# One level of Strassen's seven products for w_down, in three phases among the gate/up tiles of a decoder block

## The chip, the core and the metric

The kernel runs on one core of a Trainium2 chip. The metric is the device time of one execution in microseconds (us), as the median of several runs. The engines named below are TensorE (PE), which multiplies matrices and has a separate row for loading the stationary operand (PEld), VectorE (DVE), ScalarE (ACT), GpSimd (POOL) and SyncE (SP). SP's queue issues the transfers between the chip's memory (HBM) and the on-chip memory (SBUF); matmuls write to PSUM, of eight banks of 512 fp32 columns.

## The reference

One decoder layer on 512 tokens of width 1024, in float32: a mixer of state-space heads and pooling groups, a cross-attention into 256 memory tokens, a gated feed-forward, each behind an RMS norm and with a residual sum, and a final norm. What the change touches is the last part:

```python
D_MODEL, SEQ, D_FF = 1024, 512, 2816

def rmsnorm(x, g):
    y = x * lax.rsqrt(jnp.mean(x * x, axis=-1, keepdims=True) + EPS)
    return y * g

def swiglu(u, w_gate_up, w_down):
    gate, up = jnp.split(u @ w_gate_up, 2, axis=-1)
    return (jax.nn.silu(gate) * up) @ w_down

h = h + hybrid_mixer(rmsnorm(h, mix_norm), ...)
h = h + memory_cross_attention(rmsnorm(h, xattn_norm), rmsnorm(mem, mem_norm), ...)
h = h + swiglu(rmsnorm(h, ffn_norm), w_gate_up, w_down)
return rmsnorm(h, final_norm)
```

## The kernel before

**Layout.** Features lie on partitions, in tiles of 128; the 512 tokens are the free dimension. The residual stream is eight tiles h1 of 128 x 512. Every product is done in a reduced float32 format (fp32r) to nearly full precision: each operand is split in a high part (a cast) and a low part (the rest), and each product of 128 x 128 by 128 x 512 is three matmuls, high x high, high x low and low x high (`mm3`, L105).

**Weights.** They come in units of 128 x 1024 fp32. `load_unit` (L137) starts a transfer from SP into a raw buffer (three of them, `wb[0]`), and `split_unit` (L143) makes the high part `whi` by a cast on ACT (four buffers) and the low part `wlo` by a subtraction on DVE (five buffers). `advance` (L1091) runs one slot ahead of the matmuls.

**The order.** `SPEC` is a list of slots; each slot names items such as `f:3` (gate/up tile 3) or `d:2` (output tile 2 of the down projection). An item has matmuls (`mm`) and work behind them (`post`). The recording order of slot t is: the posts of slot t - 1, the weights of slot t + 1, then the matmuls of slot t. A scheduler then sets the order on each engine. Every engine, and SP's queue, works its own list in order.

**Feed-forward.** `i_ff` (L975) makes a tile of 128 features of the gate and of the up projection (48 matmuls), multiplies both by the norm's factor, applies SiLU and multiplies (DVE), and splits the result into `ffh` and `ffl`. There are 22 such tiles. Then `i_down` (L998) makes eight output tiles of 128 x 512 over all 22 reduction tiles, 66 matmuls each, with the weights stationary. Its post adds the tile to h1, squares it on ACT and adds the squares up on DVE. The eighth tile is cut in two halves of 256 tokens (`dA`, `dB`), and `i_final` (L1033) makes the final norm for each half: a matmul with ones sums the squares over features (`Rms`, L213), and ACT and DVE make the factor. The first half's norm and output run beside the second half's matmuls.

**What the loads before the feed-forward need.** The pairs of state-space heads, `P:0` to `P:7`, hold their decay matrices in buffers tagged m and m2, two of each. `i_op` (L740) loads the residual's x tiles again from SP, one per output tile.

Of the kernel before, what the change touches and what calls it, by code (L numbers as in the profile page):

```python
# [7 lines left out]
F32 = mybir.dt.float32  # L8
# [38 lines left out]
]  # L47
# [3 lines left out]
def hybrid_block(ctx: ExitStack, tc: tile.TileContext, a: dict, out: bass.AP,  # L51
                 act_bufs=69, la=1, wb=(3, 4, 5), eng="", dact=(0, 1), raw_n=6, warm=12, spec=None, start=START, smm=START_MM, hu=1, dbg=None):
    nc = tc.nc
# [80 lines left out]
    def add_unit(key, ap, n):  # L134
        units[key] = (ap, n)

    def load_unit(key):  # L137
        ap, n = units[key]
        raw = wraw.tile([P, 1024], F32, tag="raw", name=nm("raw"))
        nc.sync.dma_start(raw[:, :n], ap)  # L140
        ready[key] = raw

    def split_unit(key):  # L143
        n = units[key][1]
        raw = ready[key]
        hi = whi_p.tile([P, 1024], F32R, tag="hi", name=nm("whi"))
        lo = wlo_p.tile([P, 1024], F32R, tag="lo", name=nm("wlo"))
        nc.scalar.copy(hi[:, :n], raw[:, :n])  # L148
        yield
        nc.vector.tensor_tensor(out=lo[:, :n], in0=raw[:, :n], in1=hi.bitcast(F32)[:, :n], op=ALU.subtract)  # L150
        ready[key] = (hi, lo)
        yield
# [42 lines left out]
    DS = ((0, 8), (8, 16), (16, 22))  # L195
    for m in range(8):
        for i, (k0, k1) in enumerate(DS):
            add_unit(("d", m, i), a["w_d"][m, :, k0 * P:k1 * P], (k1 - k0) * P)

# [13 lines left out]
    class Rms:  # L213
# [27 lines left out]

        def first(self):
            self.ps = PS(self.base)
            self.pre = rms4[0].pre
            nc.tensor.matmul(self.ps[:, :self.n], ones, st[self.acc][:, self.o:self.o + self.n],
                             start=True, stop=False)

        def second(self, sq):
            nc.tensor.matmul(self.ps[:, :self.n], ones, sq, start=False, stop=True)

        def post(self):
# [31 lines left out]

# [1 line left out]
    rms1 = Rms("r1", "xacc", parts=False)  # L285

    def i_start(its):
# [58 lines left out]
        return it  # L346

    def i_out():
        def post():
            for m in range(8):  # L350
                nc.sync.dma_start(out[m * P:(m + 1) * P, :], st["hg", m][0].bitcast(F32))

        return Item(post=post)

# [122 lines left out]

# [1 line left out]
    def i_btm(g):  # L479
# [203 lines left out]

# [1 line left out]
    def i_v(m):  # L685
# [73 lines left out]
    rms3 = Rms("r3", "h2acc")  # L759
    rms4 = [Rms("r4a", "h3acc", 256, 0, False), Rms("r4b", "h3acc", 256, 256, False)]  # L760
    rmsm = Rms("rm", "macc", MEM)
# [19 lines left out]

# [1 line left out]
    def i_memld():  # L783
# [189 lines left out]

# [1 line left out]
    def i_ff(j):  # L975
        it = Item(keys=[("g", j), ("u", j)])

        def mm():
            xs = [st["fg", k] for k in range(8)]
            it.pg = PS("g")  # L980
            proj(it.pg, ready[("g", j)], xs)
            it.pu = PS("u")
            proj(it.pu, ready[("u", j)], xs)

        def post():
            yield from need("r3")
            g = mul("g", it.pg, st["r3",])
            nc.scalar.activation(g, g, AF.Silu)
            u = mul("u", it.pu, st["r3",])
            yield  # L990
            nc.vector.tensor_tensor(out=u, in0=u, in1=g, op=ALU.mult)
            yield
            yield from splits([("ff", j)], [("ff", 512)], [u])

        it.mm, it.post = mm, post
        return it

    def i_down(m, half=None, ks=(0, JF)):  # L998
        it = Item(keys=[("d", m, i) for i in range(3)] if not half and ks[0] == 0 else [])
        cs = slice(0, S) if half is None else slice(256 * half, 256 * half + 256)  # L1000
        last = ks[1] == JF

        def mm():
            if ks[0] == 0:
                st["dps", half] = PS("d")
            ps = st["dps", half][:, cs]
            for i, (k0, k1) in enumerate(DS):
                wh, wl = ready[("d", m, i)]
                for k in range(max(k0, ks[0]), min(k1, ks[1])):
                    o = slice((k - k0) * P, (k - k0 + 1) * P)  # L1010
                    xh, xl = st["ff", k]
                    mm3(ps, wh[:, o], wl[:, o], xh[:, cs], xl[:, cs], k == 0, k == JF - 1)
            if last and half is not None:
                rms4[half].first()

        def post():
            h = st["h1", m][:, cs]
            nc.vector.tensor_tensor(out=h, in0=h, in1=st["dps", half][:, cs], op=ALU.add)
            if half is not None:
                sq = T("sq", n=256)  # L1020
                st["sq7", half] = sq
                st["h3acc", "sq"] = nc.scalar.activation(sq, h, AF.Square)
            else:
                sq_acc("h3acc", h)
                nc.scalar.activation(h, h, AF.Identity, scale=col(V_FIN + m))
                if m == 6:
                    drain(rms4[0].split(KT - 1))

        it.mm = mm
        it.post = post if last else None  # L1030
        return it

    def i_final(half):  # L1033
        cs = slice(256 * half, 256 * half + 256)

        def post():
            yield from rms4[half].post()
            r = st["r4" + "ab"[half],]
            for m0, n in ((0, 1), (1, 1), (2, 2), (4, 2), (6, 2)):
                o = T("out").rearrange("p (m t) -> p m t", m=2)  # L1040
                for i in range(n):
                    m = m0 + i
                    h = st["h1", m][:, cs]
                    if m < 7:
                        nc.vector.tensor_tensor(out=o[:, i, :], in0=h, in1=r, op=ALU.mult)
                    else:
                        nc.vector.scalar_tensor_tensor(out=o[:, i, :], in0=h, scalar=col(V_FIN + 7), in1=r,
                                                       op0=ALU.mult, op1=ALU.mult)
                nc.sync.dma_start(out[m0 * P:(m0 + n) * P, cs].rearrange("(m p) t -> p m t", p=P), o[:, 0:n, :])
                yield  # L1050

        return Item(mm=lambda: rms4[half].second(st["sq7", half]), post=post)

    def rm(r):
        return Item(mm=r.mm, post=r.post)

# [1 line left out]
    x0, x1 = i_xbc(0), i_xbc(1)  # L1058
# [3 lines left out]
    def num(t):  # L1062
# [7 lines left out]
        "r2": lambda: rm(rms2), "rt": i_r2t, "q": i_q, "S": i_score, "T": i_ptr, "V": i_v2, "O": i_pv,  # L1070
        "o": i_o, "r3": lambda: rm(rms3), "f": i_ff, "d": i_down, "dA": lambda: i_down(7, 0),
        "dB": lambda k0, k1: i_down(7, 1, (k0, k1)), "F": i_final, "out": i_out,
    }
# [89 lines left out]
def _pack(inp):  # L1163
# [31 lines left out]
    w_u = np.stack([f(t) for t in u])  # L1195
    w_d = np.stack([f(mtile(g["w_down"], m)) for m in range(8)])
    dtp = np.zeros((KT, P, 96), z32)
# [24 lines left out]
    vecs[:, V_RC:V_RC + 16] = (1.0 / np.arange(1, 17)).astype(z32)  # L1222
    return {"xT": f(x.T), "memT": f(mem.T), "vecs": vecs, "w_dt": w_dt, "w_u": w_u, "w_d": w_d}

# [15 lines left out]
```

## Time and profile before

| what | us |
| --- | --- |
| runs of the kernel (3) | 832.57, 830.25, 832.3 |
| median | 832.3 |
| span of the profiled execution, first to last instruction | 828.6 |
| granted TensorE clock over the span | 0.996 of full |

The profile is of one execution. Of this execution the span is recorded; the time of a run lies a few us above it, 3.7 us at the median. The lines that matter are shown in the prediction. To read them: L106 is line 106 of the kernel; `d<-t_ffh,whi` is a matmul into PSUM tile d from the moving tile t_ffh and the stationary tile whi; x198 is a count; in rows of groups the busy time is followed by the mean duration of one in ns, then the idle time before the group and what ended it. Matmul records overlap, so their spacing has to be read from their starts.

### The profile page before, as it was taken

What the parts mean: (1) busy time and instruction counts of PE and PEld (TensorE: products, weight loads), DVE (VectorE), ACT (ScalarE), POOL (GpSimd) and SP (SyncE); (2) the same over time, 40 slices, a digit from 0 to 9 for tenths busy, and PEclk for the clock granted to TensorE, in tenths of its full rate; (3) what the DMA queues carried; (4) which work ended last, traced back from release to release, by engine and by line L of the source; (5) the groups of instructions that cost most, each with busy time, mean ns of one, the idle gap of its engine ahead of it and who ended that gap; (6) DMA issues with size and microseconds to landing.
All of it is one profiled execution on the core that took longest, in us unless ns stands there. A gap on an engine that the chain in (4) does not pass through costs nothing.

```text
span 828.6 us, 10051 instructions
## 1 busy us (share of the span) xinstructions
PE 816.6 (99%) x3926; PEld 686.8 (83%) x3926; DVE 505.5 (61%) x727; ACT 388.3 (47%) x600; POOL 1.7 (0%) x10
## 2 busy tenths in 40 slices
PE   9999999999999999999999999999999999999995
PEld 7878888888888899888888888888888888888885
DVE  7989978999866885447646544444444444232324
ACT  8668699477844563345534532233222332232221
POOL 0000000000000000000000000000000000000000
PEclk9999999999999999999999999999999999999998
DMA  7243514243262244223322233222323223333302
GB/s 264 78 152 102 171 62 144 70 163 120 103 221 86 76 155 160 92 77 127 102 77 91 87 102 102 94 88 98 102 101 102 88 85 96 96 96 102 100 1 101
DMA packets 31246, 89.77 MB, mean 108 GB/s; under 512 B 3664, under 2 KB 8144, under 8 KB 31200
## 3 DMA queue, kind: packets, MB, share of 16 engines
q1 hardware_dynamic: 31200, 89.15, 33.0%
q8 instruction: 30, 0.49, 0.3%
q14 instruction: 16, 0.13, 0.1%
HBM read 87.01 MB, written 2.13 MB: 108 GB/s over the span
## 4 chain that ended last, share of the span: by engine, by line
PE 91%; DVE 4%; ACT 2%; DMA 1%; issue 1%; SPq 0%; DVEq 0%
PE d L106 5%; PE d L108 5%; PE d L107 5%; PE u L107 5%; PE g L107 5%; PE u L106 5%; PE g L106 5%; PE u L108 5%; PE g L108 5%; PE v L107 2%; PE v L108 2%; PE v L106 2%; PE op L106 2%; PE op L108 2%; PE q L106 2%; PE q L107 2%
## 5 line engine op out<-in xcount | busy, mean ns | idle before, releaser
L148 ACT CAST whi<-raw 128x1024 fp32r<-128x1024 f32 x144 | 149.4, 1040 | 332.4 <-issue 108.0
L150 DVE TENSOR_TENSOR wlo<-raw,whi 128x1024 fp32r<-128x1024 f32 x144 | 173.5, 1207 | 109.6 <-ACT whi L148 109.5
L106 PE MATMUL d<-t_ffh,whi 128*128 128x512 f32 (+1 forms) x198 | 72.7, 367 | 0.0
L108 PE MATMUL d<-t_ffh,wlo 128*128 128x512 f32 (+1 forms) x198 | 72.3, 365 | 0.0
L107 PE MATMUL d<-t_ffl,whi 128*128 128x512 f32 (+1 forms) x198 | 72.3, 365 | 0.0
L106 PE MATMUL g<-t_fgh,whi 128*128 128x512 f32 x176 | 68.5, 389 | 0.0
L107 PE MATMUL g<-t_fgl,whi 128*128 128x512 f32 x176 | 68.5, 389 | 0.0
L108 PE MATMUL g<-t_fgh,wlo 128*128 128x512 f32 x176 | 68.5, 389 | 0.0
L106 PE MATMUL u<-t_fgh,whi 128*128 128x512 f32 x176 | 68.5, 389 | 0.0
L107 PE MATMUL u<-t_fgl,whi 128*128 128x512 f32 x176 | 68.5, 389 | 0.0
L108 PE MATMUL u<-t_fgh,wlo 128*128 128x512 f32 x176 | 68.5, 389 | 0.0
L277 DVE TENSOR_TENSOR t_u<-u,t_r3t 128x512 f32<-128x512 f32 x22 | 15.2, 691 | 69.0 <-PE u L108 69.0
L107 PEld LDWEIGHTS d<-t_ffl,whi 128*128 128x128 f32 x198 | 37.3, 189 | 6.1
L106 PEld LDWEIGHTS d<-t_ffh,whi 128*128 128x128 f32 x198 | 37.3, 189 | 6.0
L108 PEld LDWEIGHTS d<-t_ffh,wlo 128*128 128x128 f32 x198 | 37.3, 189 | 6.0
L277 DVE TENSOR_TENSOR t_g<-g,t_r3t 128x512 f32<-128x512 f32 x22 | 15.2, 691 | 44.3 <-PE g L108 44.3
L106 PEld LDWEIGHTS g<-t_fgh,whi 128*128 128x128 f32 x176 | 33.1, 188 | 6.9
L108 PEld LDWEIGHTS u<-t_fgh,wlo 128*128 128x128 f32 x176 | 33.1, 188 | 6.9
L106 PEld LDWEIGHTS u<-t_fgh,whi 128*128 128x128 f32 x176 | 33.0, 188 | 6.9
L107 PEld LDWEIGHTS g<-t_fgl,whi 128*128 128x128 f32 x176 | 33.1, 188 | 6.8
L108 PEld LDWEIGHTS g<-t_fgh,wlo 128*128 128x128 f32 x176 | 33.0, 188 | 6.8
L107 PEld LDWEIGHTS u<-t_fgl,whi 128*128 128x128 f32 x176 | 33.0, 188 | 6.8
(342 smaller groups left out, 1828.0 us busy)
## 6 DMA issues: line engine op xcount, KB each, us to landing
raw<-w_u SPq DMA_DIRECT2D x120, 512.0 KB, 3.3
raw<-w_d SPq DMA_DIRECT2D x16, 512.0 KB, 3.6
t_x<-xT SPq DMA_DIRECT2D x16, 256.0 KB, 4.7
t_abc<-d_acs SPq DMA_DIRECT2D x16, 256.0 KB, 4.8
raw<-w_d SPq DMA_DIRECT2D x8, 384.0 KB, 3.2
t_E<-d_acs SPq DMA_DIRECT2D x16, 96.0 KB, 4.7
outT<-t_out SPq DMA_DIRECT2D x6, 256.0 KB, 2.3
raw<-w_u SPq DMA_DIRECT2D x4, 256.0 KB, 5.6
```

The costliest lines, as they stand in the source:

```text
L106: nc.tensor.matmul(ps, whi, xhi, start=start, stop=False)
L107: nc.tensor.matmul(ps, whi, xlo, start=False, stop=False)
L108: nc.tensor.matmul(ps, wlo, xhi, start=False, stop=stop)
L148: nc.scalar.copy(hi[:, :n], raw[:, :n])
L150: nc.vector.tensor_tensor(out=lo[:, :n], in0=raw[:, :n], in1=hi.bitcast(F32)[:, :n], op=ALU.subtract)
L277: nc.vector.tensor_tensor(out=t, in0=in0, in1=in1, op=ALU.mult)
```

## The change

w_down (2816 x 1024) is cut in two along the reduction and in two along the output, the activations in two along tokens (256 each) and along the reduction: 22 reduction tiles become 11 pairs i. Seven products of sums of quadrants take the place of eight. The products are accumulated in the form in which partial sums are shared: bank pair A takes products 1, 6, 7 and 4 on top of each other and is read out after each; bank pair B takes 5 and 3, pair C takes 2. `INTO` says where each reading is added or subtracted. The activations are now the stationary operand (128 tokens), and the weights move (512 output columns), so outputs have tokens on partitions.

The eleven pairs are worked in three phases, as soon as the gate/up tiles that they need are there: pairs 0 to 3 after f:8, pairs 4 to 7 after f:16, pairs 8 to 10 after f:21. In the code `d:p.f` is product f of phase p, `d:2.f.0` and `d:2.f.1` are its parts for pairs 8 and 9 and for pair 10; `DOWN` groups two pairs to a chunk c of weights. `H:c.r` transposes the residual to tokens on partitions: token tile c, half r of the output columns.

The quadrants of w_down come as units `w_s`. Quadrants 11 and 12 go to the buffers m and m2; 21 goes to a raw buffer, and a transfer issued from POOL adds 22 (for product 5) or 11 (for product 7) to it in place. The operands of products 6 and 3 are made from these by sums on DVE. `forms` makes the sums of the activations.

```diff
+DOWN = [(0, 1), (2, 3), (4, 5), (6, 7), (8, 9), (10,)]
-    ... "f:0 r3", "f:1", ... "f:21",
-    "d:0", "d:1", "d:2", "d:3", "d:4", "d:5", "d:6", "dA", "dB:0.6 F:0", "dB:6.22", "F:1",
+    ... "f:0 r3 H:0.0", "f:1 H:0.1", ... "f:7 H:1.3", "f:8",
+    "d:0.1", "d:0.2", "d:0.6", "d:0.5", "d:0.7", "d:0.3", "d:0.4",
+    "f:9", ... "f:16",
+    "d:1.1", "d:1.2", "d:1.6", "d:1.5", "d:1.7", "d:1.3", "d:1.4",
+    "f:17", "f:18", "f:19", "f:20", "f:21 G",
+    "d:2.1.0", "d:2.2.0", "d:2.5.0", "d:2.1.1 d:2.2.1", "d:2.6", "d:2.5.1", "d:2.3", "d:2.7", "d:2.4", "",
-    ... wb=(3, 4, 5) ...
+    ... wb=(6, 4, 5) ...
+    def load_strassen(key):
...
+        if f == 1:
+            sw[c, 1] = plain("11", "m")
+        elif f == 2:
+            sw[c, 2] = plain("12", "m2")
+        elif f == 4:
+            sw[c, 4] = plain("22")
+        elif f == 7 or (c, 5) not in sw:
+            g = 7 if f == 7 else 5
+            sw[c, g] = plain("21")
+            nc.gpsimd.dma_start(sw[c, g][:, :n], quad(c, "11" if g == 7 else "22"), accum_op=ALU.add)
     def split_unit(key):
+            if f == 6:
+                nc.vector.tensor_tensor(out=sw[c, 6][:, :n], in0=sw[c, 6][:, :n], in1=sw[c, 5][:, :n], op=ALU.add)
...
+            elif f == 3:
+                nc.vector.tensor_tensor(out=sw[c, 3][:, :n], in0=sw[c, 3][:, :n], in1=sw[c, 6][:, :n], op=ALU.add)
...
+    def forms(i, FA, FB):
+        H1 = cast("xh", FA)
+        H4 = cast("xq", FB[:, hi_], lo_)
+        M = T("x57")
+        nc.vector.tensor_tensor(out=M[:, lo_], in0=FA[:, lo_], in1=FB[:, lo_], op=ALU.subtract)
+        nc.vector.tensor_tensor(out=M[:, hi_], in0=FB[:, hi_], in1=FB[:, lo_], op=ALU.subtract)
...
+    BANK = {1: "A", 6: "A", 7: "A", 4: "A", 5: "B", 3: "B", 2: "C"}
+    INTO = {1: (0, 0, 1), 2: (0, 0, 1), 6: (0, 1, 1), 5: (1, 1, -1), 7: (1, 1, -1), 3: (0, 1, 1), 4: (1, 0, -1)}
+    def i_down(p, f, part=None):
...
+            for tt in range(2):
+                ts_ = slice(tt * P, (tt + 1) * P)
+                for c, i, n in pairs:
+                    for x, w in ((xh, wh), (xl, wh), (xh, wl)):
+                        nc.tensor.matmul(it.ps[tt], x[:, ts_], w[:, ws], start=first, ...)
...
+        def post():
+            for tt in range(2):
+                h = st["h", 2 * k + tt, r]
+                nc.vector.tensor_tensor(out=h, in0=h, in1=it.ps[tt], op=ALU.add)
...
+                if last and f in (2, 3):
+                    half_done(2 * k + tt, r)
+                elif last and f in (7, 4):
+                    final(2 * k + tt)
+    def half_done(c, r):
+        nc.scalar.activation(T("sq"), h, AF.Square, accum_out=q)
+        nc.vector.tensor_tensor(out=h, in0=h, in1=st["G"][r], op=ALU.mult)
+    def final(c):
+        half_done(c, 1)
...
+        ln = nc.scalar.activation(y, v, AF.Ln)
+        nc.scalar.activation(y, y, AF.Exp, scale=-0.5)
...
+            nc.sync.dma_start(out[rows, 512 * r:512 * r + 512], o)
```

The order of the instructions shows three places. The first is on DVE, around gate/up tile f:8, behind which phase 0 begins. Before, its list had two multiplications by the norm's factor (`t_r3t`), two low halves of weights, the product and the split of the activation (`g_4964` and `u_4989` are the gate and up sums of f:8):

```order
L277 TENSOR_TENSOR t_g_5014<-g_4964,t_r3t_4439 128x512
L150 TENSOR_TENSOR wlo_5022<-raw_4956,whi_5021 128x1024
L277 TENSOR_TENSOR t_u_5017<-u_4989,t_r3t_4439 128x512
L991 TENSOR_TENSOR t_u_5017<-t_u_5017,t_g_5014 128x512
L150 TENSOR_TENSOR wlo_5031<-raw_5019,whi_5030 128x1024
L181 TENSOR_TENSOR t_ffl_5033<-t_u_5017,t_ffh_5026 128x512
```

Now the same tile is followed by sums and splits of quadrants and by the reads of bank A (`dA`) after product 1:

```order
L315 TENSOR_TENSOR t_g_5146<-g_5096,t_r3t_4452 128x512
L196 TENSOR_TENSOR wlo_5152<-wq_4981,whi_5151 128x1024
L189 TENSOR_TENSOR wq_4981<-wq_4981,wq_4884 128x1024
L315 TENSOR_TENSOR t_u_5149<-u_5121,t_r3t_4452 128x512
L1026 TENSOR_TENSOR t_fa_5154<-t_u_5149,t_g_5146 128x256
L1026 TENSOR_TENSOR t_fb_5155<-t_u_5149,t_g_5146 128x256
L196 TENSOR_TENSOR wlo_5160<-wq_4991,whi_5159 128x1024
L189 TENSOR_TENSOR wq_4991<-wq_4991,wq_4899 128x1024
L196 TENSOR_TENSOR wlo_5195<-wq_4884,whi_5194 128x1024
L1130 TENSOR_TENSOR t_hT_4445<-t_hT_4445,dA_5163 128x512
L1130 TENSOR_TENSOR t_hT_4532<-t_hT_4532,dA_5163 128x512
```

The sums for product 3 (`wq_4981`, `wq_4991`) have moved ahead of the phase's first product, and the reads of bank A stand behind the first split of product 6 (`wlo_5195`).

The second place is the end of TensorE's list. Before, the last 66 matmuls had 256 columns and the norm's sums behind them. Its last rows were:

```order
L108 MATMUL d_6666<-t_ffh_5890,wlo_6518 128x256
L106 MATMUL d_6666<-t_ffh_5968,whi_6517 128x256
L107 MATMUL d_6666<-t_ffl_5975,whi_6517 128x256
L108 MATMUL d_6666<-t_ffh_5968,wlo_6518 128x256
L245 MATMUL r4b_6759<-t_h3acc_6052,ones 128x256
```

Now, in phase 2, two matmuls of product 7 (`whi_6896`) stand between the last part of product 5 (`whi_6850`) and product 3 (`whi_6877`):

```order
L1117 MATMUL dB_6797<-whi_6850,t_xl_6749 128x512
L1117 MATMUL dB_6797<-wlo_6851,t_xh_6742 128x512
L1117 MATMUL dA_6754<-whi_6896,t_xh_6428 128x512
L1117 MATMUL dA_6754<-whi_6896,t_xl_6436 128x512
L1117 MATMUL dB_6796<-whi_6877,t_xq_6416 128x512 x2
L1117 MATMUL dB_6796<-wlo_6878,t_xq_6416 128x512
```

The rest of product 7 follows product 3, and product 4 follows it directly, into the same bank pair. The third place is SP's list, where the x tiles of the residual are loaded for the mixer's output projection. Before:

```order
L574 DMA t_E_2064<-d_acs 64x384 x2
L745 DMA t_x_456_2183<-xT 128x512
L745 DMA t_x_457_2186<-xT 128x512
L745 DMA t_x_458_2188<-xT 128x512
L140 DMA raw_2279<-w_u 128x1024
```

And now, with the quadrants 11 (`wq_4884`) and 12 (`wq_4981`) of phase 0's first chunk:

```order
L605 DMA t_E_2070<-d_acs 64x384 x2
L155 DMA wq_4884<-w_s 128x1024
L155 DMA wq_4981<-w_s 128x1024
L776 DMA t_x_459_2189<-xT 128x512
L776 DMA t_x_460_2192<-xT 128x512
L776 DMA t_x_461_2194<-xT 128x512
L175 DMA raw_2285<-w_u 128x1024
```

Two transfers of 512 KB have come ahead of the x tiles; they go into buffers of tags m and m2 that the matmuls of pair 6 read before.

More of the change, by code (lines that the diff above doesn't have):

```diff
@@ L194, in hybrid_block @@
             idx += 1
[L195 to L198, printed above, removed]
+    QUAD = {"11": 0, "12": 1, "21": 2, "22": 3}
+    for c, pairs in enumerate(DOWN):
+        for f in (1, 2, 3, 4, 5, 6, 7):
+            add_unit(("d", c, f), None, len(pairs) * 512)
+    sw = {}
     st = {}
@@ L240, in mm @@
                 nc.tensor.matmul(self.ps[:, :n], ones, self.src, start=True, stop=True)
[L242 to L249, printed above, removed]
         def post(self):
@@ L346, in i_start @@
         return it
[L348 to L353, printed above, removed]
     def i_norm(*ks):
@@ L992, in post @@
             yield
-            yield from splits([("ff", j)], [("ff", 512)], [u])
+            if c == 1:
+                yield from forms(i, *st["F", i])
         it.mm, it.post = mm, post
         return it
[L998 to L1001, printed above, removed]
-        def mm():
[L1004 to L1014, printed above, removed]
-        def post():
[L1017 to L1022, printed above, removed]
-            else:
[L1024 to L1031, printed above, removed]
@@ new lines, in i_down, with mm @@
+    def i_down(p, f, part=None):
+        chunks = [2 * p, 2 * p + 1] if part is None else [2 * p + part]
+        it = Item(keys=[("d", c, f) for c in chunks])
+        full = part != 0
+        pairs = [(c, i, n) for c in chunks for n, i in enumerate(DOWN[c])]
+        def mm():
+            bank = BANK[f]
+            if f in (1, 2, 5) and part != 1:
+                if bank == "A":
+                    t = psum.tile([P, 1024], F32, tag="pd", name=nm("dA"), bufs=1)
+                    st[bank] = [t[:, 0:512], t[:, 512:1024]]
+                else:
+                    st[bank] = [PS("d" + bank) for _ in range(2)]
+            it.ps = st[bank]
+            for tt in range(2):
+                ts_ = slice(tt * P, (tt + 1) * P)
+                first = f in (1, 2, 5) and part != 1
+                for c, i, n in pairs:
+                    wh, wl = ready[("d", c, f)]
+                    ws = slice(512 * n, 512 * n + 512)
+                    xh, xl = st["X", f, i]
+                    for x, w in ((xh, wh), (xl, wh), (xh, wl)):
+                        nc.tensor.matmul(it.ps[tt], x[:, ts_], w[:, ws], start=first,
+                                         stop=(c, i, n) == pairs[-1] and x is xh and w is wl, skip_group_check=True)
+                        first = False
+        def post():
+            r, k, sign = INTO[f]
+            last = p == 2
+            if last and f == 2:
+                st["pre"] = nc.scalar.preload_act_table_set("natural_log_exp_and_others")
+                after(st["pre"], st["silu"])
+            for tt in range(2):
+                h = st["h", 2 * k + tt, r]
+                if sign > 0:
+                    nc.vector.tensor_tensor(out=h, in0=h, in1=it.ps[tt], op=ALU.add)
+                else:
+                    nc.vector.tensor_tensor(out=h, in0=h, in1=it.ps[tt], op=ALU.subtract)
+                if last and f in (2, 3):
+                    half_done(2 * k + tt, r)
+                elif last and f in (7, 4):
+                    final(2 * k + tt)
+            yield
+        it.mm, it.post = mm, post if full else None
+        return it
@@ L1195, in _pack @@
     w_u = np.stack([f(t) for t in u])
-    w_d = np.stack([f(mtile(g["w_down"], m)) for m in range(8)])
+    wd = g["w_down"].reshape(JF // 2, 2, P, 2, 512)
+    w_s = np.zeros((len(DOWN), 4, P, 1024), z32)
+    for c, pairs in enumerate(DOWN):
+        for q, (r, k) in enumerate(((0, 0), (0, 1), (1, 0), (1, 1))):
+            for n, i in enumerate(pairs):
+                w_s[c, q, :, 512 * n:512 * n + 512] = wd[i, k, :, r]
     dtp = np.zeros((KT, P, 96), z32)
@@ L1238 @@
     res = run_bass_kernel_spmd(nc, [arrays], core_ids=[0])
-    return np.ascontiguousarray(res.results[0]["outT"].T)[None]
+    return np.ascontiguousarray(res.results[0]["out"])[None]
```

131 lines of the change are left out of this document (104 added, 27 removed), and 4 rows, old and new, of the table SPEC.

## The prediction

> **What bounds the kernel now.** I read the page first: its span, the engines' busy time and the shares of the chain.
>
> ```profile
> span 828.6 us, 10051 instructions
> PE 816.6 (99%) x3926; PEld 686.8 (83%) x3926; DVE 505.5 (61%) x727; ACT 388.3 (47%) x600; POOL 1.7 (0%) x10
> ...
> PE 91%; DVE 4%; ACT 2%; DMA 1%; issue 1%; SPq 0%; DVEq 0%
> ```
>
> TensorE is busy in all but 12 us and carries 91% of the chain. A busy row does not prove that TensorE works at its peak, so next come the windows by stage (columns: length, then busy time and instructions of PE, weight loads, DVE, ACT, POOL, then clock, DMA share, GB/s). The rows are attention, gate/up, down projection, tail.
>
> ```profile
> 254.00:457.00 203.00, 203.00 (x1051) 174.36 (x1050) 126.94 (x194) 95.13 (x154) 0.00 (x0) 1.00 0.31 104
> 457.00:696.60 239.60, 239.60 (x1058) 198.45 (x1057) 113.29 (x136) 76.43 (x95) 0.00 (x0) 1.00 0.29 96
> 696.60:818.10 121.50, 121.50 (x600) 103.40 (x599) 38.85 (x49) 32.72 (x40) 0.00 (x0) 1.00 0.26 76
> 818.10:828.60 10.50, 1.19 (x5) 0.39 (x3) 4.58 (x12) 1.31 (x3) 0.00 (x0) 0.65 0.43 147
> ```
>
> From 254 us to 818 us TensorE never idles and the clock is full. In gate/up 1056 of the 1058 are 512-column matmuls: 239.6 / 1056 = 0.227 us from start to start (a record of 0.39 us overlaps its neighbour). So time falls here only by fewer or shorter matmuls, and DVE (38.85 of 121.5 us) and ACT (32.72) have room in the down projection. The timeline of TensorE gives its parts.
>
> ```profile
> 696.60 0.39 PE L106 MATMUL d<-t_ffh,whi 128*128 128x512 f32 x1
> ...
> 801.32 0.28 PE L106 MATMUL d<-t_ffh,whi 128*128 128x256 f32 x1
> ...
> 817.88 0.28 PE L108 MATMUL d<-t_ffh,wlo 128*128 128x256 f32 x1
> 818.00 0.38 PE L245 MATMUL r4b<-t_h3acc,ones 128*128 128x256 f32 x1
> ```
>
> Seven whole tiles take 696.60 to 801.32, 104.72 us for 7 x 66 = 462 matmuls. The eighth, cut in halves of 256 columns, takes 801.32 to 818.00, 16.68 us, with the first norm's sums between. From 818.00 to 828.57 the tail runs, 10.57 us.
>
> **The change: matmuls removed.** Seven products, two token tiles of 128, 11 pairs of reduction tiles, three matmuls each: 7 x 2 x 11 x 3 = 462, all 512 columns wide. That is exactly the count of the seven whole tiles. What was stationary now moves and the other way round; the rows of V, which stood so already, show the same duration:
>
> ```profile
> L106 PE MATMUL d<-t_ffh,whi 128*128 128x512 f32 x154 | 59.9, 389 | 0.0
> L108 PE MATMUL v<-whi,t_mn 128*128 128x512 f32 x32 | 12.5, 389 | 0.0
> ```
>
> So 104.72 us stay and the eighth tile's 16.68 us go: **-16.7 us**.
>
> **Transposes added.** Eight items H of four 128x128 transposes stand behind f:0 to f:7. In attention eight such transposes took:
>
> ```profile
> 360.24:361.03 0.79, 0.79 (x8) 0.79 (x8) 0.00 (x0) 0.00 (x0) 1.00 0.25 99
> L929 PE MATMUL pT<-ident,t_p 128*128 128x128 f32 x8 | 1.0, 272 | 0.0
> ```
>
> 0.79 / 8 = 0.099 each, so 32 cost **+3.2 us**, all on the bound engine. The record is 272 ns but eight of them end to end take 0.79 us. The Trainium skill, "TensorE: Matmul & The Clock Gate", Part 4, puts a transpose in a kernel at about 275 ns and says that the full clock does not engage for it. By that, 32 would cost 8.8 us as an estimate; this trace agrees with the duration of one, not with that spacing, and its clock stays 1.00 there.
>
> **Work on DVE and ACT.** The costs come from these rows:
>
> ```profile
> L150 DVE TENSOR_TENSOR wlo<-raw,whi 128x1024 fp32r<-128x1024 f32 x42 | 51.3, 1222 | 29.4 <-ACT whi L148 29.4
> L148 ACT CAST whi<-raw 128x1024 fp32r<-128x1024 f32 x41 | 43.2, 1054 | 139.3 <-issue 50.1 <-PE d L107 41.1 <-PE g L107 40.4
> L181 DVE TENSOR_TENSOR t_ffl<-t_u,t_ffh 128x512 fp32r<-128x512 f32 x15 | 10.3, 684 | 0.0
> L1018 DVE TENSOR_TENSOR t_x<-t_x,d 128x512 f32<-128x512 f32 x7 | 4.8, 687 | 17.3 <-PE d L108 17.3
> L1018 DVE TENSOR_TENSOR t_x<-t_x,d 128x256 f32<-128x256 f32 x2 | 0.8, 420 | 6.4 <-PE d L108 6.4
> L173 ACT CAST t_ffh<-t_u 128x512 fp32r<-128x512 f32 x15 | 9.4, 625 | 9.8 <-DVE t_u L991 9.8
> ```
>
> A gate/up tile lasts 48 x 0.227 = 10.9 us. DVE has two splits (2.44), two multiplications (1.38), the product in two halves (0.84), and half of one pair's forms: five operations of 256 columns and three of 512 are 2.10 + 2.05 = 4.15, so 2.1. Sum 6.8 of 10.9. A whole product lasts 24 x 0.227 = 5.45 us; DVE has two splits and two bank reads, 2.44 + 1.37 = 3.8; ACT two casts, 2.1. Two quadrant sums of 1.22 us for each of products 6 and 3 stand, by the order of DVE, before f:8's second multiplication or just behind it, so they are past before the products begin to need DVE. Forms on ACT are 3 x 0.63 + 0.4 = 2.3 us a pair. All of that is hidden by matmuls; uncovered it would be some 4 us a product.
>
> What can show are the buffers: with four high halves, product n+1's cast waits for product n-1. I laid the rows of DVE in their order against the matmuls with these durations. In phases 0 and 1 every weight stands 2 us or more before its product and every read of bank A ends over 2 us before the next product adds to it, since a product on another bank lies between: **0**. In phase 2 the pieces are of 6, 12 and 18 matmuls (1.4, 2.7, 4.1 us), and product 4 adds to bank A directly behind product 7. There I find three waits: 0.2 us before the first matmul of product 7 (its high half and the read of A), 0.75 before product 3 (read of bank B, fourth in DVE's row of reads), 0.5 before product 4 (DVE still splits its weights when product 7's first token tile ends). Behind the waiting matmul stands the rest of TensorE, so they are paid: **+1.5 us**; bounds 0 (scheduled as if free) and 4, six evacuations of 0.69 us in full.
>
> **Loads.** Sums of quadrants are made by twelve accumulating transfers that POOL issues behind plain ones. No trace shows one. Rows near it:
>
> ```profile
> raw<-w_d SPq DMA_DIRECT2D x16, 512.0 KB, 3.6
> ...
> raw<-w_u SPq DMA_DIRECT2D x4, 256.0 KB, 5.6
> ```
>
> Bounds 3.6 us (the same bytes) and 11.2 (two at the slowest rate); I take 3.6. The first sum's buffer is free when f:4's first split ends, so its plain load lands about when f:5 begins, and DVE adds it in the second half of f:7: some 28 us, and 37 us for two in a row. In either bound it is hidden: **0**. The Trainium skill, "DMA: Bandwidth & Descriptors", Anatomy of one DMA, gives 2.0 us + bytes / 436e3 for a transfer issued by GpSimd, an estimate of 3.2 us here; no run shows it yet, and the sum stays.
>
> SP now sends the first quadrants ahead of the residual's x tiles, into buffers that pair 6's matmuls must leave first.
>
> ```profile
> t_x<-xT SPq DMA_DIRECT2D x16, 256.0 KB, 4.7
> ...
> 203.40 1.48 SPq L745 DMA_DIRECT2D t_x<-xT x3
> ...
> 211.44 0.28 PE L108 MATMUL pd<-mh,t_xcl 128*128 128x256 f32 x1
> ...
> 227.72 0.69 DVE L751 TENSOR_TENSOR t_x<-t_x,op 128x512 f32<-128x512 f32 x1
> ```
>
> The x tiles go out at about 212.6 instead of 203.4 and land, 4.7 us later and behind two transfers of 512 KB, by 224, before DVE added them at 227.72. Cost **0** with op's matmuls as the cover; without it up to the 9 us of the delay. Three more raw buffers let SP run three units further ahead at the start, before TensorE needs them: **0**.
>
> **The tail.** The norm's matmuls go; sums come from ACT's accumulator, per token tile.
>
> ```profile
> 818.20 0.42 DVE L1018 TENSOR_TENSOR t_x<-t_x,d 128x256 f32<-128x256 f32 x1 [0.52 <-PE d L108]
> ...
> L907 ACT ACTIVATION_READ_ACCUMULATOR t_p<-sc,nb,r2s 128x1 f32 x16 | 3.2, 201 | 0.0
> L902 DVE SCALAR_TENSOR_TENSOR nb<-mx,r2s 128x2 f32<-128x2 f32 x8 | 1.3, 158 | 0.2
> ...
> L1025 ACT ACTIVATE t_x<-t_x,vec 128x512 f32<-128x512 f32 x7 | 5.1, 725 | 0.2
> ...
> 825.11 0.37 SPq L1049 DMA_DIRECT2D outT<-t_out x1
> ```
>
> From the end of the last matmul's issue: 0.2 us to DVE's read (818.00 to 818.20) and 0.69 for it. Then DVE holds two gain multiplications, 1.3, and about nine steps on single columns of 0.16 to 0.2 between ACT's Ln and Exp (0.2 each), about 1.9, and ACT scales the last half, 0.7: 4.8. Two more issues at SP, 0.4 each, put the last one at 5.2; from such an issue to the end took 828.57 - 825.11 = 3.46. So 8.7 instead of 10.57: **-1.9**; bounds 7.5 (steps of half the length) and 10.6 (as long as now).
>
> **Sum.** -16.68 + 3.16 + 1.5 - 1.9 = -13.9 us. The span of 828.6 becomes 814.7. The runs shown have their median at 832.3, 3.7 above that span, which I leave as it is: 832.3 - 13.9 = **818.4 us**.
>
> **Rivals.** First, *waits at every hand-over*. If each of the 21 products and parts that follow another in a phase waits 0.5 us, as I find for the last one, it is 10.5 instead of 1.5: 827.4. For it: product n+1's high half waits for product n-1's last matmul, and DVE is at 3.8 of 5.45 us. Against: 2 us of room in the timetable, and a TensorE that waited for nothing from 254 to 818 us with two splits in 10.9 us.
>
> Second, *the tail does not shrink*. Products 7 and 4 close all four token tiles within 8 us, where now one half is finished behind the other half's matmuls. If DVE still has all of token tiles 2 and 3 in hand when product 4 ends (two gain multiplications, two scalings and nine small steps, 1.4 + 1.0 + 1.4 = 3.8 us), the tail is 12.5: 822.2, and more if ACT's steps between them come late.
>
> Third, *slower: the accumulating transfers are the bound*. POOL's twelve run one after another; if one takes a us, the two sums that a phase needs first are late by 2a - 37, and as DVE works in order, everything behind them waits, three times. The gain of 13.9 is gone at 3(2a - 37) = 13.9, a = 20.8 us; at a = 25 it is 39 us: 857. For it: nothing in the trace shows such a transfer, and POOL ran ten small instructions. Against: 20.8 is nearly six times 3.6 and almost twice the upper bound of 11.2.
>
> That the change doesn't do what it says would need the 462 matmuls to be slower than 0.227 us in their new form; the V rows speak against that. It counts under the remainder.
>
> **Chances.** Forecast 0.72; waits at every hand-over 0.10; long tail 0.09; slow transfers 0.05; remainder (a shift in an earlier stage, either way) 0.04. The forecast's own bounds are -2.7 (no waits, shortest tail) and +4.4 (4 us of waits, tail as now). The range 814.5 to 825.0 holds these but for their far ends, and the long tail: 0.8. A measurement can tell about 0.3%, 2.5 us, from no change. Faster by more takes the forecast, the long tail, 0.05 of the hand-overs and 0.01 of the rest: 0.87. Within 0.3%: the other 0.05 of the hand-overs (waits of over 0.6 us) and 0.01, together 0.06. Slower: 0.05 and 0.02, together 0.07.
>
> **What would show it.** In the profile after: 462 matmuls of 512 columns by name dA, dB, dC, none of 256, and gate/up at 0.227 us. Transposes hT of about 0.4 us per four. The list of TensorE's waits holds less than 2 us in all, on dA and dB in the last 20 us; a long list of waits for DVE across the phases would be the first rival. Waits of DVE for a DMA in front of f:8's multiplication would be the third. The last matmul's issue to the end: 8.7 us. The prediction is wrong if matmuls with moving weights are slower, or if a read of bank A stands late in DVE's row in phases 0 or 1.

## The result and the profile after

| what | before | after |
| --- | --- | --- |
| runs (4 each) | 832.57, 830.25, 832.3, 833.04 | 819.43, 818.77, 820.34, 819.1 |
| median, us | 832.43 | 819.26 |
| span of the profiled execution, us | 828.6 | 817.3 |

The medians lie 13.2 us apart; the ratio of the runs is 0.9849, with a 95% interval of 0.9835 to 0.9863. The change makes the kernel about 1.5% faster. The first lines of the page, the chain's shares and two of the new groups of transfers (count, KB each, median us to landing) answer to the page of before.

```profile
span 817.3 us, 10121 instructions
PE 803.8 (98%) x3818; PEld 672.9 (82%) x3818; DVE 579.9 (71%) x882; ACT 418.0 (51%) x656; POOL 12.1 (1%) x22
...
PE 96%; DVE 2%; DMA 1%; ACT 0%; issue 0%; SPq 0%; DVEq 0%; ACTq 0%
...
raw<-w_s SPq DMA_DIRECT2D x15, 512.0 KB, 3.4
...
raw<-w_s POOLq DMA_DIRECT2D x10, 512.0 KB, 5.8
```

TensorE is busy 12.8 us less (816.6 to 803.8), DVE 74.4 us more. The windows give the stages: the first two rows are phases 0 and 1, then phase 2 (from f:21's last matmul to the end of the last matmul's issue), then the tail. Columns as in the prediction.

```profile
558.94:597.00 38.06, 38.06 (x170) 31.52 (x169) 25.59 (x30) 14.80 (x15) 0.00 (x0) 1.00 0.51 165
...
684.06:722.10 38.04, 38.04 (x170) 31.50 (x169) 25.57 (x30) 14.77 (x15) 0.00 (x0) 1.00 0.45 152
...
776.38:807.86 31.48, 29.26 (x127) 23.15 (x125) 28.43 (x56) 16.45 (x33) 0.00 (x0) 1.00 0.03 12
807.86:817.30 9.44, 0.16 (x1) 0.00 (x0) 4.54 (x14) 3.48 (x10) 0.00 (x0) 0.74 0.48 186
```

In phases 0 and 1 TensorE does not idle: 168 matmuls at 0.2267 us are 38.09 us, and from its first start to the first start of the stage behind it each phase takes 38.08 in the trace (the windows begin 0.16 us late). DVE has a third of the time free. Phase 2 has 126 matmuls, 28.56 us, and lasts 31.48: 2.92 us too long. There DVE is busy for 28.43 us, 90%. The list of TensorE's waits (us in total, times, longest) names the two places (first and third row); before had none over 0.6 us but the one on `ones` at the start.

```profile
PE dA L1117 <- ACT t_sq L1152: 1.5, 1, 1.5
PE warm L370 <- DVE ones L93: 1.2, 1, 1.2
PE dA L1117 <- DVE t_hT L1130: 0.7, 1, 0.7
```

The timelines of TensorE and of DVE at these places (start, length, instruction, count, idle time before and what ended it):

```profile
792.57 0.39 PE L1117 MATMUL dB<-wlo,t_xh 128*128 128x512 f32 x1
793.70 0.47 PE L1117 MATMUL dA<-whi,t_xh 128*128 128x512 f32 x1 [0.74 <-DVE t_hT L1130]
794.01 0.40 PE L1117 MATMUL dA<-whi,t_xl 128*128 128x512 f32 x1
794.25 0.69 PE L1117 MATMUL dB<-whi,t_xq 128*128 128x512 f32 x2
...
796.13 0.39 PE L1117 MATMUL dB<-wlo,t_xq 128*128 128x512 f32 x1
...
799.76 0.39 PE L1117 MATMUL dA<-wlo,t_xh 128*128 128x512 f32 x1
...
801.80 0.39 PE L1117 MATMUL dA<-wlo,t_xh 128*128 128x512 f32 x1
803.66 0.47 PE L1117 MATMUL dA<-whi,t_xh 128*128 128x512 f32 x1 [1.47 <-ACT t_sq L1152]
...
807.63 0.39 PE L1117 MATMUL dA<-wlo,t_xh 128*128 128x512 f32 x1
```

```profile
792.28 1.28 DVE L1130 TENSOR_TENSOR t_hT<-t_hT,dA 128x512 f32<-128x512 f32 x2
793.48 1.28 DVE L1132 TENSOR_TENSOR t_hT<-t_hT,dB 128x512 f32<-128x512 f32 x2
...
796.56 0.69 DVE L1130 TENSOR_TENSOR t_hT<-t_hT,dB 128x512 f32<-128x512 f32 x1
...
802.22 1.29 DVE L1132 TENSOR_TENSOR t_hT<-t_hT,dA 128x512 f32<-128x512 f32 x2 [0.44 <-PE dA L1117]
...
808.06 1.29 DVE L1132 TENSOR_TENSOR t_hT<-t_hT,dA 128x512 f32<-128x512 f32 x2 [0.93 <-PE dA L1117]
```

From the end of the last issue (792.572 + 0.227, to the nanosecond of the trace) to product 7's first matmul at 793.704 are 0.91 us, and to product 4's (801.80 + 0.23 to 803.66) 1.63. The second wait is put down to a square on ACT, but product 4 does not use it; what ends just before 803.66, by 0.15 us, is DVE's second read of bank A, at 803.51. Product 7's first matmul stands as close behind the second read of product 6's sum (792.28 + 1.28 = 793.56). And the read at 802.22 is odd: product 7's first token tile had its last matmul at 799.76, DVE stood idle for 0.44 us before 802.22, and yet both reads start only when the second token tile is complete. The same at 808.06, in the tail. Bank B is read half by half (796.56, after a last matmul at 796.13). Bank A is one PSUM tile of 1024 columns over two banks, B is two tiles of 512. That is theory W: the program waits for a tile as a whole, reads and matmuls alike. Its rival is Q: DVE, 90% busy, is simply late, whatever the tile. Both can be at work: product 6's last matmul ended at 791.83 (791.44 + 0.39), but DVE was at weight splits until 792.3 before it read.

### The profile page after: what moved, and what is told of

Its sections match the earlier page's. It is cut to its first block, busy times and chain, and to the rows that moved or that the text cites. A ratio compares the mean times of both kernels' runs of the same rounds, so it can differ in the third digit from the quotient of the medians.

```text
span 817.3 us, 10121 instructions
## 1 busy us (share of the span) xinstructions
PE 803.8 (98%) x3818; PEld 672.9 (82%) x3818; DVE 579.9 (71%) x882; ACT 418.0 (51%) x656; POOL 12.1 (1%) x22
## 4 chain that ended last, share of the span: by engine, by line
PE 96%; DVE 2%; DMA 1%; ACT 0%; issue 0%; SPq 0%; DVEq 0%; ACTq 0%
PE dA L1117 7%; PE g L112 5%; PE g L110 5%; PE u L112 5%; PE g L111 5%; PE u L110 5%; PE u L111 5%; PE dB L1117 4%; PE v L111 2%; PE v L112 2%; PE v L110 2%; PE xbc L112 2%; PE xbc L111 2%; PE xbc L110 2%; PE dC L1117 2%; PE z L110 2%
## 5 line engine op out<-in xcount | busy, mean ns | idle before, releaser
L194 ACT CAST whi<-raw 128x1024 fp32r<-128x1024 f32 (+1 forms) x138 | 143.4, 1042 | 239.9 <-issue 79.6
L196 DVE TENSOR_TENSOR wlo<-raw,whi 128x1024 fp32r<-128x1024 f32 (+1 forms) x138 | 166.6, 1210 | 72.3 <-ACT whi L194 71.8
L315 DVE TENSOR_TENSOR t_u<-u,t_r3t 128x512 f32<-128x512 f32 x22 | 15.2, 691 | 57.7 <-PE u L112 57.7
L194 ACT CAST whi<-wq 128x1024 fp32r<-128x1024 f32 (+1 forms) x24 | 23.5, 981 | 44.1 <-PE u L111 18.1
L1117 PE MATMUL dA<-whi,t_xh 128*128 128x512 f32 x88 | 34.5, 392 | 2.2 <-ACT t_sq L1152 1.5
L1117 PE MATMUL dA<-wlo,t_xh 128*128 128x512 f32 x88 | 34.3, 389 | 0.0
L1117 PE MATMUL dA<-whi,t_xl 128*128 128x512 f32 x88 | 34.2, 389 | 0.0
L196 DVE TENSOR_TENSOR wlo<-wq,whi 128x1024 fp32r<-128x1024 f32 (+1 forms) x24 | 27.2, 1132 | 5.5 <-ACT whi L194 5.3
L1041 ACT CAST t_xh<-t_x 128x512 fp32r<-128x512 f32 x22 | 13.7, 623 | 23.1 <-DVE t_x L1051 12.1
```

Source lines behind the costliest of these rows:

```text
L315: nc.vector.tensor_tensor(out=t, in0=in0, in1=in1, op=ALU.mult)
L1041: nc.scalar.copy(h if w is None else h[:, w], src)
L1117: nc.tensor.matmul(it.ps[tt], x[:, ts_], w[:, ws], start=first, stop=(c, i, n) == pairs[-1] and x is xh and w is wl, skip_group_check=True)
```

## The experiments

All times are medians; the kernel after is at 819.26, the kernel before at 831.73 to 832.43, as it ran beside each. The kernel after was not run again beside the experiments, so a difference between two versions of 0.7 us, as much as the kernel before moves from set to set, is no more than a hint; what a part of the kernel gains is read from the windows.

**Bank A as two tiles.**

```diff
-                    t = psum.tile([P, 1024], F32, tag="pd", name=nm("dA"), bufs=1)
-                    st[bank] = [t[:, 0:512], t[:, 512:1024]]
+                    ...
+                    st[bank] = [late["a"].tile([P, 512], F32, tag="a%d" % i, name=nm("dA"), bufs=1) for i in range(2)]
```

> Bank A is one PSUM tile of 1024 columns in the changed kernel; here it is two tiles of 512 columns, and nothing else is edited (the scheduler then places some bank reads ahead of weight splits). Theory W (the tile is waited for as a whole: the read of its first token tile waits for the matmuls of both, and product 7's and product 4's first matmul for both reads): the gaps of 0.91 us before product 7 and 1.63 us before product 4 fall to 0.3 us or less each, the tail from the end of the last matmul's issue falls from 9.4 to about 8.8 us, and the time by 2 to 2.7 us, to 816.6 to 817.3. Theory Q (DVE's queue is simply late in phase 2, whatever the tile): gaps of 2 to 3 us in all stay, perhaps before other products, and the time stays within 0.7 us of 819.3.

Measured: 817.64 us, ratio to before 0.9833 (0.9818 to 0.9847), 1.6 us less than after. The windows of phase 2 and of the tail, then two places of DVE's timeline, then the same places of TensorE's:

```profile
776.87:806.75 29.88, 29.14 (x127) 23.31 (x125) 28.41 (x57) 16.29 (x34) 0.00 (x0) 1.00 0.00 1
806.75:815.50 8.75, 0.15 (x1) 0.00 (x0) 3.99 (x14) 3.68 (x10) 0.00 (x0) 0.68 0.63 240
```

```profile
793.58 1.28 DVE L1137 TENSOR_TENSOR t_hT<-t_hT,dB 128x512 f32<-128x512 f32 x2
...
801.11 0.68 DVE L199 TENSOR_TENSOR wlo<-raw,whi 128x512 fp32r<-128x512 f32 x1
801.72 0.68 DVE L1137 TENSOR_TENSOR t_hT<-t_hT,dA 128x512 f32<-128x512 f32 x1
```

```profile
793.87 0.39 PE L1122 MATMUL dA<-whi,t_xl 128*128 128x512 f32 x1
794.32 0.73 PE L1122 MATMUL dB<-whi,t_xq 128*128 128x512 f32 x2
...
801.48 0.39 PE L1122 MATMUL dA<-wlo,t_xh 128*128 128x512 f32 x1
802.54 0.47 PE L1122 MATMUL dA<-whi,t_xh 128*128 128x512 f32 x1 [0.67 <-DVE t_numbers L1176]
```

DVE's read of the first token tile now begins at 801.72, before product 7's last matmul of the second has ended (801.48 + 0.39). Phase 2 is 1.6 us shorter, the gap before product 7 is gone, and the tail is 8.75 us. That is W. The scheduler also placed some reads ahead of weight splits here, so the 1.6 us belong to the two tiles together with that order. Before product 4 there are still 0.83 us: the read stood behind a weight split that ended at 801.8, although its data had been there since about 800. That part is Q. And a start 0.22 us late (0.45 instead of 0.23 from 793.87 to 794.32) has appeared before product 3, directly behind the first read of bank B, which the trace ends at 794.26.

**Product 7 ahead of product 3.** The kernel after, the run before this one and two new ones make a square of tile and order.

```diff
-    ... "d:2.6", "d:2.5.1", "d:2.3", "d:2.7", "d:2.4", "",
+    ... "d:2.6", "d:2.5.1", "d:2.7", "d:2.3", "d:2.4", "",
-                if last and f in (2, 3):
+                if last and f in (2, 7):
                     half_done(2 * k + tt, r)
-                elif last and f in (7, 4):
-                    final(2 * k + tt)
+                elif last and f in (3, 4):
+                    final(2 * k + tt, r)
```

With two tiles:

> On top of bank A as two tiles: in phase 2 product 7 stands ahead of product 3, so that product 3's 18 matmuls (4.1 us) lie between product 7 and product 4; the closing of token tiles 2 and 3 moves from product 7's read to product 3's. With two tiles the gap that was left was 0.83 us before product 4, where DVE's read of bank A stood behind weight splits. If that hand-over was the cause, the gap goes and the time falls by 0.5 to 0.8 us, to 816.9. If DVE is simply short of time in the last 25 us, the wait turns up before product 7 (its splits are now due 4 us earlier) and the time stays or rises by up to 1.5 us.

With the one tile:

> Product 7 ahead of product 3 as in the run before, but with bank A as the one tile of 1024 columns that the changed kernel has. If the whole tile is what is waited for, product 7 now stands directly behind the 6 matmuls of product 5's second part and waits for both reads of product 6, 0.7 to 1.5 us; the gap of 1.63 us before product 4 goes, because product 3 lies between; phase 2 lasts 29.3 to 30.1 us, and the time is about 818.0. If only the order mattered and not the tile, phase 2 lasts 28.6 us as in the run before, and the time is 817.0.

| us | time | phase 2 | tail |
| --- | --- | --- | --- |
| one tile, 3 then 7 (the kernel after) | 819.26 | 31.48 | 9.44 |
| two tiles, 3 then 7 | 817.64 | 29.88 | 8.75 |
| one tile, 7 then 3 | 819.15 | 29.67 | 10.31 |
| two tiles, 7 then 3 | 817.02 | 28.62 | 9.44 |

The ratios to before of the last two are 0.9846 (0.9832 to 0.9859) and 0.9817 (0.9799 to 0.9836). The windows of phase 2, first with one tile and then with two:

```profile
777.82:807.49 29.67, 28.94 (x127) 23.31 (x125) 26.91 (x51) 15.11 (x31) 0.00 (x0) 1.00 0.00 1
```

```profile
777.78:806.40 28.62, 28.62 (x127) 23.46 (x125) 27.73 (x53) 15.59 (x32) 0.00 (x0) 1.00 0.00 1
```

Both are needed to rid phase 2 of its waits. With one tile the wait before product 4 goes and product 7 waits instead, as W has it:

```profile
794.01 0.39 PE L1117 MATMUL dB<-wlo,t_xh 128*128 128x512 f32 x1
795.13 0.47 PE L1117 MATMUL dA<-whi,t_xh 128*128 128x512 f32 x1 [0.73 <-DVE t_hT L1130]
```

With two, phase 2 has no wait left, 28.62 us for 126 matmuls. But the gain of 1.3 us there is half lost in the tail: DVE, busy in 27.73 of 28.62 us, now carries its arrears past the last matmul, 18 instructions with 4.56 us of work instead of the 14 with 3.99 of the other order:

```profile
806.36:815.80 9.44, 0.14 (x1) 0.00 (x0) 4.56 (x18) 4.27 (x12) 0.00 (x0) 0.68 0.58 222
```

The 818.0 expected of the one tile was a miss: I had not seen that its tail would grow.

**The gain in the same operation as the scale.** On top of both:

```diff
     def half_done(c, r, gain=True):
...
+        if gain:
             nc.vector.tensor_tensor(out=h, in0=h, in1=st["G"][r], op=ALU.mult)
...
     def final(c, r):
-        half_done(c, r)
+        half_done(c, r, False)
...
-            if r == 0:
+            if r != last:
                 nc.scalar.activation(o, o, AF.Copy, scale=w)
...
-                nc.vector.tensor_scalar(out=o, in0=o, scalar1=w, scalar2=None, op0=ALU.mult)
+                nc.vector.scalar_tensor_tensor(out=o, in0=o, scalar=w, in1=st["G"][r], op0=ALU.mult, op1=ALU.mult)
```

> On top of two tiles and product 7 first: in the last column half of each token tile the gain is multiplied together with the scale, in one operation on DVE behind the small steps, instead of one multiplication ahead of them and one behind. DVE is busy in 27.7 of phase 2's 28.6 us there, and in the tail the gain of the last half (0.69 us, begun at 809.15) stands on the way to the last scaling. If DVE's queue sets the tail, it falls from 9.44 to 8.3 to 8.8 us and the time by 0.6 to 1.1 us, to 816.2; if the chain through ACT sets it, the time stays within 0.4 us of 817.0.

The half that closes last now always goes to DVE, the other to ACT. Measured: 816.05 us, ratio 0.9807 (0.9794 to 0.9821), and a tail of 8.57:

```profile
805.83:814.40 8.57, 0.16 (x1) 0.00 (x0) 3.90 (x12) 3.59 (x10) 0.00 (x0) 0.65 0.64 245
```

So 0.9 us of that tail were DVE's queue. This version beats both kernels: 3.2 us below the kernel after, with ratios whose intervals do not overlap.

**The transposes left out.**

```diff
-                nc.tensor.transpose(pt[:, i * P:(i + 1) * P], st["h1", 4 * r + i][:, c * P:(c + 1) * P], ident)
-            nc.scalar.copy(st["h", c, r], it.ps)
+            nc.scalar.copy(st["h", c, r], st["h1", 4 * r + c])
```

> The 32 transposes of the residual are left out: ACT copies tiles of h1 as they stand, so the residual that is added is not turned. Theory by spacing (each four cost what they take end to end, 0.36 to 0.40 us, 3.2 us in all as the prediction has it): the time falls by 3.2 us, to 816.1. Theory with the hand-over (the matmul behind each four also starts late, 0.47 us per four as read in gate/up): it falls by 3.8 us, to 815.5. By the duration of the records (0.27 us each) it would be 8.7 us, 810.6.

Measured: 815.28 us, ratio 0.9805 (0.9791 to 0.982): 4.0 us for 32, nearer the theory with the hand-over; but the two theories lie only 0.6 us apart, and what decides is the timeline of TensorE in the kernel after:

```profile
467.87 0.60 PE L1081 MATMUL hT<-ident,t_x 128*128 128x128 f32 x4
468.23 0.48 PE L110 MATMUL g<-t_fgh,whi 128*128 128x512 f32 x1
468.55 0.39 PE L111 MATMUL g<-t_fgl,whi 128*128 128x512 f32 x1
```

Four transposes hold TensorE for 0.36 us, and the matmul behind them for 0.32 instead of 0.23: 0.45 for each four, 3.6 for eight. In the group of all such matmuls it can be seen as a mean of 394 ns against 389:

```profile
L110 PE MATMUL g<-t_fgh,whi 128*128 128x512 f32 x176 | 69.3, 394 | 0.0
```

All eight places look alike (0.31 to 0.32). Why that matmul is longer was not tried.

**An eighth product, by repetition and in earnest.**

```diff
-                for c, i, n in pairs:
+                for c, i, n in pairs * (2 if f == 2 else 1):
...
```

> Product 2's matmuls are issued twice in each phase, 66 more of 512 columns on bank C, with no more splits or reads; the result is changed by product 2 added once more. If the number of matmuls is what Strassen saves, the time rises by 66 x 0.2267 = 15.0 us, to 834.2, less up to 1 us of waits that the added time covers for DVE. If TensorE had been waiting for DVE or ACT all along the phases, the added matmuls would hide in part: under 10 us.

Measured: 834.44 us, ratio 1.0033 (1.002 to 1.0046): 15.2 us for 66 matmuls. The waits on bank A stayed (0.5 and 1.5 us in its list). So matmuls added to the phases cost their full time; nothing hides them.

The second kernel multiplies quadrants without Strassen: units for the four quadrants, hidden values split as they are, four token tiles per quadrant, all eight banks in use.

```diff
-    BANK = {1: "A", 6: "A", 7: "A", 4: "A", 5: "B", 3: "B", 2: "C"}
+                    st["D", r] = [PS("dA") for _ in range(4)]
...
+            for tt in range(4):
...
+                for c, g, i, n in pairs:
+                    xh, xl = st["X", tt // 2, i]
+                    o = 256 * ((g - 1) % 2) + P * (tt % 2)
+                        nc.tensor.matmul(it.ps[tt], x[:, o:o + P], w[:, ws], start=first, ...)
```

> The same layout and phases (tokens stationary, output with tokens on partitions, transposed residual) with the eight ordinary products of quadrants instead of Strassen's seven: 528 matmuls instead of 462, plain casts of the hidden values in place of the forms, 24 weight pieces instead of 42 and no sums of quadrants. Theory by count: +15.0 us for 66 matmuls, less the 2.5 us of gaps in phase 2 where DVE now has less to do, 831.5 to 834.5: about the time of the kernel before, so that the layout alone gains nothing and its transposes eat what the tail gives. Rival: the layout itself gains (fewer weight switches, shorter tail): below 829.

Measured: 831.45 us, ratio 0.9998 (0.9987 to 1.0009). The windows of its last phase (144 matmuls) and tail:

```profile
787.65:820.33 32.68, 32.68 (x145) 26.84 (x143) 16.98 (x36) 11.40 (x25) 0.00 (x0) 1.00 0.09 33
820.30:829.50 9.20, 0.15 (x1) 0.00 (x0) 4.54 (x14) 3.48 (x10) 0.00 (x0) 0.70 0.30 114
```

The layout alone, with phases, transposes and the new tail, gains nothing that can be told from no change. Its last phase has no wait at all, with DVE at half load. From it to the kernel after are 12.2 us, where 66 matmuls are 15.0: the whole gain of the change is Strassen's count, less 2.8 us, about the 2.9 that phase 2 waits.

**Accumulating transfers twice and four times over.**

```diff
-            nc.gpsimd.dma_start(sw[c, g][:, :n], quad(c, "11" if g == 7 else "22"), accum_op=ALU.add)
+            for _ in range(4):
+                nc.gpsimd.dma_start(sw[c, g][:, :n], quad(c, "11" if g == 7 else "22"), accum_op=ALU.add)
```

The first run has 2 in place of the 4.

> Each accumulating transfer is issued twice in a row (its quadrant is added twice, so the result is changed). One took 5.8 us from issue to landing in the changed kernel. If they run one after another, a sum of quadrants is ready after 11.6 us, and the two sums that a phase needs first after 23 us, inside the 37 us that the prediction gave them: the time stays within 0.8 us of 819.3. If the room were already used up (the third rival), it would rise by 3 x 11.6 = 35 us.

> Each accumulating transfer is issued four times in a row (its quadrant is added four times, so the result is changed). If they run one after another at 5.8 us, a = 23.2 us for a sum, and the prediction's formula 3 x (2a - 37) gives 28 us more, about 847; the first waits would be DVE's, for a DMA, ahead of the sums of quadrants. If the room is larger than 37 us (for instance because the plain load goes out earlier than the prediction has it), little: under 5 us. If they overlap, nothing.

Measured: 819.45 (ratio 0.9848, 0.9829 to 0.9867) and 820.05 us (0.9851, 0.9832 to 0.9869), no difference from after. With four, those on one buffer did run one after another, but two buffers went side by side. The timeline of POOL in the kernel with four has the second and third issue for the first sum (520.34, 525.82) around the first for the second sum (522.49):

```profile
520.34 0.86 POOL L168 DMA_DIRECT2D raw<-w_s  x1 [4.73 <-DMA raw<-w_s]
522.49 0.85 POOL L168 DMA_DIRECT2D raw<-w_s  x1 [1.29 <-DVE wlo L197]
525.82 0.86 POOL L168 DMA_DIRECT2D raw<-w_s  x1 [2.48 <-DMA raw<-w_s]
```

The landings in the trace put the first sum at 514.6 to 542.3 and the second at 522.5 to 556.6. DVE did wait for the second, as its timeline shows (first the kernel with four, then the kernel after):

```profile
556.66 1.23 DVE L186 TENSOR_TENSOR wq<-wq,raw 128x1024 f32<-128x1024 f32 x1 [3.70 <-DMA raw<-w_s]
```

```profile
552.50 1.22 DVE L185 TENSOR_TENSOR wq<-wq,raw 128x1024 f32<-128x1024 f32 x1
```

In the kernel after, DVE reached this sum at 552.50 with the data there. With eight transfers ahead of it from 514.6 on, it came 4.2 us later. TensorE's list of waits names no transfer in either: the sum is for product 6, whose first matmul is at 558.78 + 2 x 5.44 = 569.7. DVE is some 10 us ahead of TensorE at this place, and the wait is absorbed there: a weight split that DVE starts at 571.10 in the kernel after starts at 571.66 here, where the phase itself began 0.4 us later, and phase 0 lasts 38.08 us in both.

**The loads' settings alone, in the kernel before.**

```diff
-                 ... wb=(3, 4, 5), ...
+                 ... wb=(6, 4, 5), ...
-    nc = bacc.Bacc("TRN2", target_bir_lowering=False, num_devices=1)
+    nc = bacc.Bacc("TRN2", target_bir_lowering=False, num_devices=1, dynamic_dma_scratch_size=4096)
```

> The kernel before with six raw buffers for weights instead of three and the changed kernel's descriptor setting, nothing else. The prediction has these at 0 in the earlier stages. In the traces gate/up begins 0.26 us earlier in the changed kernel: if that is the buffers' doing, the time falls by 0.3 us from that of the kernel before; if it is chance of one execution, within 0.5 us either way. A loss of over 1 us would mean that the change pays for its loads in a stage that I have not looked at.

Measured: 831.25 us, ratio 0.999 (0.9979 to 1.0001): nothing that can be told from no change. Whether 0.3 us are in it stays open.

## Why the prediction was right, and where its sizes were off

The mechanism was right: one product in eight saved, at the old rate, and the rest hidden. Its terms by the runs:

| term, us | prediction | measured | from |
| --- | --- | --- | --- |
| eighth tile's matmuls | -16.7 | -16.7 | 38.08 us for 168 in phase 0; 66 more cost 15.2 |
| 32 transposes | +3.2 | +3.6 to +4.0 | timeline; run without them |
| waits in phase 2 | +1.5 | +2.9 | 31.48 - 28.56, of which 0.91 and 1.63 are the two stops |
| tail | -1.9 | -1.1 | 9.44 - 10.57 |
| loads, accumulating transfers, earlier stages | 0 | 0 to -0.3 | transfers two and four times over; six buffers |
| sum | -13.9 | -11.3 in spans | 828.6 to 817.3 |

**Matmuls.** The rows of V had shown what a matmul with moving weights costs, and that held to 0.1 us in 38.

**Transposes.** The step "0.79 / 8 = 0.099 each" took the distance inside a row of transposes; the change of pace into the matmul behind them comes on top, once for each of the eight items. The Trainium skill's 275 ns for one ("TensorE: Matmul & The Clock Gate", Part 4, for bf16; here it is fp32) is again the length of the record, 272 ns, and not its price: 8.7 us would have been saved by leaving them out, and 4.0 were.

**Waits in phase 2.** This is the mis-sized step: "I laid the rows of DVE in their order against the matmuls". I took bank A to be handed over one token tile at a time, as B is. Product 7 and product 3 together stood at 0.2 + 0.75 and cost 0.91: the stop came whole before product 7, which waits for both reads of bank A, and covered what product 3 would have waited. The first read of bank B ended in the trace at 794.16, 0.09 us before product 3's first matmul; without the stop that matmul would have been due 0.9 us earlier, and with two tiles, where product 7 does not stop, it starts 0.22 us late. The term that was too small is product 4's: 0.5 in the sum, 1.63 measured, because bank A's tile spans two banks and both reads wait for the whole of product 7, and product 4 for both reads. The remaining 0.4 of 2.92 had no term: the first matmuls of products 6, 7, 3 and 4 took 0.29 to 0.31 us to the next start instead of 0.227, 0.3 in all, two of them without a stop on record. The square of tile and order shows the parts: by the medians the tile costs 1.6 us in the one order and 2.1 in the other, and what is left of the wait before product 4 is DVE's queue. The list of waits on bank A holds 2.2 us where the forecast's sign was less than 2.

**The tail.** The sum of steps has one read behind the last matmul; the whole tile makes it two, 1.29 us instead of 0.69. That put SP's last issue 5.8 us behind the end of the last matmul's issue instead of 5.2, and from that issue to the end took 3.6 instead of 3.46: 9.44 against 8.7. With two tiles it measured 8.75. The second rival, DVE with token tiles 2 and 3 still in hand when product 4 ends, did not come true in this order: DVE's last scaling of them ended at 807.13, before the last matmul's issue ended at 807.86. With product 7 first and one tile the tail did grow, to 10.31, still short of the rival's 12.5.

**Loads.** An accumulating transfer took 5.8 us, between the bounds of 3.6 and 11.2, and above the estimate of 3.2. For the third rival the estimate of 37 us in DVE's row held: from the first issue at 514.32 to DVE's second sum at 552.50 are 38. Two of its other steps failed. "POOL's twelve run one after another" holds for one buffer only: with four transfers to a sum the first two sums took 27.7 and 34.1 us, and 42, not 62, for both. And "everything behind them waits" holds for DVE, not for TensorE, 10 us behind it. So the rival's deciding point of 20.8 us for one sum was too low: at 27.7 its formula gives 55 us, and the median was 0.8 us above the kernel after's. The x tiles went out at 212.37 (forecast 212.6) with no wait for them.

**Waits at every hand-over**, the first rival: none in phases 0 and 1.

**From the span to the median.** I kept the 3.7 us between before's median and its span. Over the 40 runs of the kernel before that ran beside the experiments, the time lies 2.1 us above the span at the median, the spans have their median at 829.8, and the smallest is 828.6: the profiled execution was as quick as any. So 1.6 us of the 3.7 were chance, a quick execution set against a median of others. With 2.1 the same sum gives 816.8, 2.5 below the measured 819.26; the errors in waits, tail and transposes (1.4 + 0.8 + 0.4 to 0.8) are what it lacks. The forecast of 818.4 came nearer than its terms deserve: that was luck. The same quick execution makes the 11.3 us of the table small. The four runs of the kernel after have their median span at 817.2, 12.6 below 829.8; where the kernel before loses 1.2 us in a usual execution was not looked at.

## What to carry to other kernels

In this kernel a PSUM tile that spans two banks was handed over as one. Where halves are produced and read in turn, look whether the tile is one: here two tiles of one bank each were worth 1.6 to 2.1 us for a few lines of code. When the bound engine has no idle time, a saving in its instructions arrives nearly in full, but look at the engine behind it in the stage with the smallest pieces: DVE had a third of its time free in two phases and a tenth in the last one, and all the waits were there. A wait that a trace does not show may stand in the shadow of one just ahead of it, and comes out when that one is removed, as product 3's did. And take the offset from span to time from several executions, not from the difference between one profile and a median.

## What the runs showed of the hardware

- A transfer that adds into SBUF took 5.8 us for 512 KB, where a plain one of the same size and stage took 3.4. Four on the same buffer ran one after another, 27.7 to 34.1 us in all; those on two buffers ran side by side.
- Behind four transposes of 128 x 128 fp32 a matmul of 512 columns held TensorE 0.32 us instead of 0.23, at full granted clock.
- The first matmul after a wait of 0.7 to 1.5 us also has a record of 0.47 us instead of 0.39, and the next one started 0.31 us behind it instead of 0.227.
